# A decoder layer with experts on one core: the end of routing rebuilt, its index partly moved among the first expert's work

## The chip, the cores and the metric

The kernel runs on one core of a Trainium2 chip. Its engines work side by side, each through its own instructions in order, and wait for each other by semaphores: TensorE (PE in the profile, its weight loads PEld), VectorE (DVE), ScalarE (ACT), GpSimd (POOL) and SyncE (SP), which issues most of the transfers; GpSimd issues the indirect ones. The metric is the time of one execution in device microseconds; lower is better.

## What is computed

One layer: differential attention with a residual (the first 600 us, not touched here), then an RMS norm and a mixture of experts. For each of 1024 tokens a group of four experts is chosen by the largest group logit, then two experts inside it; their outputs are added, weighted:

```python
logit_g = (xt @ w_group + b_group).astype(F32)
prob_g = jax.nn.softmax(logit_g, -1)
g_sel = jnp.argmax(logit_g, -1)
gate_g = jnp.take_along_axis(prob_g, g_sel[:, None], -1)
logit_e = (xt @ w_router + b_router).astype(F32).reshape(n_tok, N_GROUPS, EXPERTS_PER_GROUP)
logit_e = jnp.take_along_axis(logit_e, g_sel[:, None, None], 1)[:, 0]
top_v, top_i = lax.top_k(jax.nn.softmax(logit_e, -1), TOP_K_IN_GROUP)
top_v = top_v / jnp.sum(top_v, -1, keepdims=True)
...
    h = jax.nn.silu(jnp.einsum('nd,edf->nef', xt, w_gate[e])) * jnp.einsum('nd,edf->nef', xt, w_up[e])
    h = h * combine[:, g, :, None].astype(h.dtype)
    y = y + jnp.einsum('nef,efd->nd', h, w_down[e])
```

There are 16 experts; the model width is 1024, an expert's 512.

## The kernel before

**Routing.** The tokens come in eight tiles of 128 (t = 0 to 7). For each, `logits` multiplies on TensorE, and `route_b` (L649) works on VectorE from the logits to `sel`, the one-hot pair of chosen experts, and then to the two weights, which it writes into the last 16 columns of xn, the normalised tokens; xn goes to the DRAM table `xn_dram`, 1040 columns wide. `route_r` (L696) turns `sel` into ranks by two small matmuls (rk) with a running count. `index_masks` (L151) compares the ranks with the slots: per expert a 128 x 128 mask pm, and one for the remainders (each expert has 140 slots, 128 and 12). `index_add` (L169) multiplies the masks with token numbers on TensorE (ix) and adds the result into ia (experts) and ir (remainders). `gather_index` (L192) makes from them the row numbers gidx, and `scatter_index` (L199) the rows sidx where results are added to the output.

**The order at the end of routing.** The order is written out by hand. In `last` (L885, t = 7) masks of tile 6 that wait in a list are put one by one between the steps of `route_b` (`Interleaved`, L619). `FIRST` names the two experts whose masks and index are made early, because the first gathers need them; the masks of the other 14 come after. `warm_up` issues matmuls whose result nobody reads. `start(part)` runs pieces of the expert stage early: 6 is the gathers for the first two experts and the first remainder block (`gather`, `gather_rem`), 2 is the first low half, 4 a weight load.

**The experts.** Each has three matrices (gate, up, down) in two tiles of 1 MB, 96 tiles in a fixed order: gate 0, up 0, gate 1, down 0, up 1, gate 2, down 1 and so on, two tiles each. A tile is loaded into `raw` (eight in flight); ScalarE rounds it to the high half mH (`split_h`, L1009), and VectorE subtracts that to get the low half mL (`split_l`, L1018). For each tile TensorE makes the high products with xT (L1088) and the low ones with xb (L1094) into two PSUM tiles (gu, three buffers of this kind). A matrix's second tile begins with its low products. `add_halves` then copies on ScalarE and adds on VectorE (L1115): gt for the gate (followed by silu), ut for up, yT for down; `hidden` (L1163) multiplies gt by ut and splits the product into hx and hb. `prepare(g)` (L1121), called after tile g's products and what follows them, splits halves ahead: high ones five tiles, low ones four (`LA = 4`; three in the last third), and loads into the freed raw buffer. `xpose(n)` transposes the gathered tokens of expert n, whose parts ScalarE and VectorE then put into xT and xb. The rest of the index (`other_experts`, L954) runs inside the first expert's first gate tile.

## Time and profile before

| | |
|---|---|
| median of 3 runs | 1005.19 us (1004.71 to 1005.73) |
| profiled execution | 1005.15 us, its span 1003.4 us |
| busy: PE, DVE, ACT, POOL | 941.4 (94%), 806.6 (80%), 748.5 (75%), 325.7 (32%) us |

The span is what the profile covers; 1.75 us of the execution's time lie around it. Busy time by stretch (end of attention's output; end of routing; first expert; the experts after it):

| stretch, us | length | PE busy | DVE busy | ACT busy | PE clock granted | DMA share |
|---|---|---|---|---|---|---|
| 596 to 620 | 24 | 23.82 | 18.95 | 9.95 | 1.00 | 0.89 |
| 620 to 635 | 15 | 9.57 | 13.30 | 9.32 | 0.89 | 0.52 |
| 635 to 658 | 23 | 20.20 | 21.59 | 15.07 | 1.00 | 0.97 |
| 658 to 679 | 21 | 20.40 | 20.39 | 19.33 | 1.00 | 0.78 |
| 679 to 701 | 22 | 21.69 | 20.07 | 20.40 | 1.00 | 0.98 |

An engine that is busy almost all of a stretch sets its length, or waits for the one that does. In a timeline a row is one or several like instructions in a row: start, time to the end of the last, engine, line, operation, output <- input with their shapes, and the count; in brackets stands how long the engine was idle before it and what ended that.

### The profile page before, as it was taken

What the parts mean: (1) busy time and instruction counts of PE and PEld (TensorE: products, weight loads), DVE (VectorE), ACT (ScalarE), POOL (GpSimd) and SP (SyncE); (2) the same over time, 40 slices, a digit from 0 to 9 for tenths busy, and PEclk for the clock granted to TensorE, in tenths of its full rate; (3) what the DMA queues carried; (4) which work ended last, traced back from release to release, by engine and by line L of the source; (5) the groups of instructions that cost most, each with busy time, mean ns of one, the idle gap of its engine ahead of it and who ended that gap; (6) DMA issues with size and microseconds to landing.
All of it is one profiled execution on the core that took longest, in us unless ns stands there. A gap on an engine that the chain in (4) does not pass through costs nothing. (4 is left out here: it accounts for less than half of the span.)

```text
span 1003.4 us, 19948 instructions
## 1 busy us (share of the span) xinstructions
PE 941.4 (94%) x7241; PEld 877.4 (87%) x7241; DVE 806.6 (80%) x1719; ACT 748.5 (75%) x1577; POOL 325.7 (32%) x977
## 2 busy tenths in 40 slices
PE   8989999999999999997899998899999999999992
PEld 7879999999999999987788886789999999999981
DVE  5578878888888888885677778999899899789880
ACT  6778877878877878776643325599999999899971
POOL 3533433415352432526744521301121312121011
PEclk8999999999999999998999999999999999999996
DMA  6230110202020110311323377889999999999923
GB/s 215 85 67 1 50 36 1 85 2 85 1 64 23 33 53 2 126 47 55 116 80 117 122 271 271 299 304 323 344 343 343 337 357 348 333 334 328 336 58 53
DMA packets 75771, 161.72 MB, mean 161 GB/s; under 512 B 8713, under 2 KB 39441, under 8 KB 67473
## 3 DMA queue, kind: packets, MB, share of 16 engines
q1 hardware_dynamic: 70544, 141.87, 39.7%
q0 software_dynamic: 5120, 18.50, 7.9%
q8 instruction: 59, 0.97, 0.4%
q14 instruction: 48, 0.39, 0.1%
HBM read 139.05 MB, written 21.30 MB: 160 GB/s over the span
## 5 line engine op out<-in xcount | busy, mean ns | idle before, releaser
L310 PE MATMUL qkv<-wH,hT 128*128 128x384 f32 x1024 | 293.3, 349 | 1.7 <-ACT wH L243 1.2
L1022 DVE TENSOR_TENSOR mL<-raw,mH 128x2048 bf16<-128x2048 f32 x95 | 215.7, 2283 | 3.7 <-ACT mH L1013 3.6
L310 PEld LDWEIGHTS qkv<-wH,hT 128*128 128x128 f32 x1024 | 190.5, 191 | 4.1 <-DVE vHL L323 2.4
L1013 ACT ACTIVATE mH<-raw 128x2048 fp32r<-128x2048 f32 x95 | 177.9, 1903 | 1.2 <-POOL rs_x L57 1.2
L310 PE MATMUL qkv<-wL,hT 128*128 128x384 f32 x512 | 173.6, 339 | 0.4 <-DVE wL L244 0.4
L1088 PE MATMUL gu<-xT,mH 128*128 128x280 f32 x1024 | 155.8, 299 | 4.1 <-DVE gt L1115 1.7
L1088 PEld LDWEIGHTS gu<-xT,mH 128*128 128x128 f32 x1024 | 136.3, 189 | 4.6 <-DVE gt L1115 1.9
L405 ACT ACTIVATE st<-st,nm 128x256 f32<-128x256 f32 (+7 forms) x128 | 99.2, 775 | 51.0 <-DVE nm L401 50.2
L1219 POOL DMA_INDIRECT out_dram<-yo,sidx x20 | 31.8, 1590 | 279.4 <-ACT yo L1217 244.8
L1094 PEld LDWEIGHTS <-mL 128*128 128x128 bf16 x1536 | 93.4, 97 | 10.6
L310 PEld LDWEIGHTS qkv<-wL,hT 128*128 128x128 f32 x512 | 98.0, 191 | 0.7 <-DVE wL L244 0.7
L401 DVE CUSTOM_DVE_ANT_0 st<-sc,bias 128x256 f32<-128x256 f32 (+7 forms) x128 | 93.7, 752 | 2.4 <-PE sc L393 0.3
L426 DVE TENSOR_TENSOR pdL<-tp,pdH 128x512 bf16<-128x512 f32 (+2 forms) x96 | 50.5, 554 | 49.6 <-ACT pdH L425 49.5
L561 PE MATMUL op<-wo,oH 128*128 128x512 f32 x256 | 82.5, 404 | 2.8 <-ACT oH L546 2.0
L1088 PE MATMUL gu<-hx,mH 128*128 128x280 f32 x512 | 82.2, 303 | 2.4 <-DVE yT L1115 1.8
L334 POOL TENSOR_SCALAR ssq<-ssq 128x8 f32<-128x8 f32 x32 | 7.1, 221 | 225.3 <-DVE ssq L326 224.7
L1094 PE MATMUL gu<-xb,mL 128*128 128x140 bf16 x1024 | 80.1, 225 | 0.0
L1088 PEld LDWEIGHTS gu<-hx,mH 128*128 128x128 f32 x512 | 68.9, 189 | 4.3 <-DVE yT L1115 3.3
L392 PE MATMUL sc<-KM,AH 128*128 128x384 f32 (+4 forms) x192 | 65.1, 345 | 2.3 <-DVE KM L367 2.3
L393 PE MATMUL sc<-KM,AL 128*128 128x384 f32 (+4 forms) x192 | 64.7, 343 | 0.5 <-DVE AL L369 0.5
L561 PEld LDWEIGHTS op<-wo,oH 128*128 128x128 f32 x256 | 47.9, 193 | 12.8 <-ACT oH L546 2.2
L412 DVE SCALAR_TENSOR_TENSOR st<-st,sm,st 128x128 f32<-128x128 f32 (+3 forms) x64 | 52.5, 820 | 2.2
(238 smaller groups left out, 1961.4 us busy)
## 6 DMA issues: line engine op xcount, KB each, us to landing
raw<-in_moe_w_gate_dram SPq DMA_DIRECT2D x32, 1024.0 KB, 8.1
raw<-in_moe_w_up_dram SPq DMA_DIRECT2D x32, 1024.0 KB, 6.8
raw<-in_moe_w_down_dram SPq DMA_DIRECT2D x31, 1024.0 KB, 8.4
wraw<-in_da_w_in_dram SPq DMA_DIRECT2D x64, 192.0 KB, 3.2
out_dram<-xres SPq DMA_DIRECT2D x9, 512.0 KB, 3.9
xraw<-in_x_dram SPq DMA_DIRECT2D x8, 512.0 KB, 6.1
woraw<-in_da_w_out_dram SPq DMA_DIRECT2D x8, 512.0 KB, 3.9
xres<-in_x_dram SPq DMA_DIRECT2D x8, 512.0 KB, 4.5
```

Source lines behind the costliest of these rows:

```text
L310: pe.matmul(ps, lhsT=hT[t][:, x, c], rhs=W[w, h, c // 3][:, c % 3], start=(c == 0 and x == 0 and w == "H"), stop=(c == 7 and x == 1))
L392: pe.matmul(ps[:, k, :wc], lhsT=AH[h, t][:, c], rhs=KM[h][:, c, ks], start=True, stop=False)
L393: pe.matmul(ps[:, k, :wc], lhsT=AL[h, t][:, c], rhs=KM[h][:, c, ks], start=False, stop=True)
L401: vec.tensor_tensor_reduce(sv, tiles[c][:, :n, :wc], bv, -1.0, 3e38, OP.add, OP.min, nm[:, c:c + 1])
L405: act.activation(st[c][:, :w], st[c][:, :w], AF.Exp, scale=-1.0, bias=nm[:, c:c + 1], accum_out=sm[:, c:c + 1])
L412: vec.scalar_tensor_tensor(st[0][:, :w], st[1][:, :w], sm[:, 3:4], st[0][:, :w], op0=OP.mult, op1=OP.add)
L426: vec.tensor_sub(pl[:, g:g + n], ps[:, :n], f(ph[:, g:g + n]))
L561: pe.matmul(ps, lhsT=o[:, c], rhs=wo[4 * half + c // 2][:, w, c % 2], start=(c == 0 and o is oh and w == 0), stop=(c == NK - 1 and o is ol))
L1013: act.activation(WH[g], full[g], AF.Copy)
L1022: vec.tensor_sub(WL[g], full[g], f(WH[g]))
L1088: pe.matmul(res[i // 2][:, i % 2, :2 * CAP], lhsT=wh[:, c - c0, 128 * i:128 * i + 128], rhs=rhs[:, c].rearrange("p a b -> p (a b)"), start ...
L1094: pe.matmul(res[i // 2][:, i % 2, :CAP], lhsT=wl[:, c - c0, 128 * i:128 * i + 128], rhs=rb[:, c], start=False, stop=(last and (c0 == 0 or ...
```

## The change

At the end of routing (`last`), the masks of tile 6 no longer stand between the steps of `route_b` for tile 7 but behind it. `route_b` ends at `sel` and hands back `weights`, which now runs behind the first low half. The index of tiles 6 and 7 for the first two experts and the remainders is made in one go: each pair of matmuls adds up in PSUM (`ahead`). The first gathers take only the 1024 columns of xn, by an index multiplied by the row width (gx); the weights go to a table of their own (`wt_dram`) and are gathered from there later (`start(7)`). The output's write comes before the norm's end instead of behind the weights.

In the experts' stage the other 14 masks of tile 7 (`flush`, now `rest[0]`) run behind two low halves, and the rest of the index (`rest[1]`), the third expert's gather and the weights' gathers run at the end of up's second tile of the first expert. Low halves are made two tiles ahead up to tile 5, three up to tile 17, and from tile 18 as before.

```diff
@@ def index_add @@
+        both = [(t, pm)] if ahead is None else [ahead, (t, pm)]
         for r in parts:
             for e in r:
-                pe.matmul(ps[:, e], lhsT=pm[:, e * 128:e * 128 + 128], rhs=tokp[:, t], start=True, stop=True)
+                for u, m in both:
+                    pe.matmul(ps[:, e], lhsT=m[:, e * 128:e * 128 + 128], rhs=tokp[:, u], start=(u == both[0][0]),
+                              stop=(u == t))
...
@@ def gather_index @@
+        if apart and lo in AT:
+
+            vec.tensor_scalar(gx[:p, AT[lo]:AT[lo] + 1], u[:, :1], float(XW), None, op0=OP.mult)
+            return lambda: gather_index(lo, hi, False)
         vec.tensor_copy(gidx[:p, lo:hi], u)
...
@@ def route_b @@
-        iv.scalar_tensor_tensor(s[:, 5:6], s[:, 4:5], 1.0, s[:, 1:2], op0=OP.add, op1=OP.mult)
-        iv.reciprocal(s[:, 5:6], s[:, 5:6])
-        iv.tensor_mul(s[:, 6:7], s[:, 5:6], s[:, 4:5])
-        iv.tensor_scalar(c2, iota16, i2[:, 1:2], s[:, 6:7], op0=OP.is_equal, op1=OP.mult)
-        iv.scalar_tensor_tensor(xn[:, D:], o1, s[:, 5:6], c2, op0=OP.mult, op1=OP.add)
...
+        def weights():
+
+            v = vec if t == NT - 1 else iv
+            v.scalar_tensor_tensor(s[:, 5:6], s[:, 4:5], 1.0, s[:, 1:2], op0=OP.add, op1=OP.mult)
+            v.reciprocal(s[:, 5:6], s[:, 5:6])
+            v.tensor_mul(s[:, 6:7], s[:, 5:6], s[:, 4:5])
+            v.tensor_scalar(c2, iota16, i2[:, 1:2], s[:, 6:7], op0=OP.is_equal, op1=OP.mult)
+            v.scalar_tensor_tensor(xn[:, D:], o1, s[:, 5:6], c2, op0=OP.mult, op1=OP.add)
+            sp.dma_start(wt_dram[t * 128:(t + 1) * 128], xn[:, D:])
+
+        if t == NT - 1:
+            R[t] = sel
+            return weights
+        weights()
...
@@ def last @@
-        x_sum = xr[t]
+        sp.dma_start(out[t * 128:(t + 1) * 128], xr[t])
         times_gain(t, x2, slice(64, 128))
         vec.scalar_tensor_tensor(ss[:, 1:2], ss[:, 1:2], -0.5 / D, ss[:, 0:1], op0=OP.mult, op1=OP.add)
         R[t] = xn, rsqrt_half(ss[:, 1:2])
+        route_r(t - 1)
+        first, rest = fill[:3], fill[3:]
+        fill.clear()
+        weights = route_b(t)
         start(3)
-        route_r(t - 1)
-        rest = fill[3:]
-        del fill[3:]
-        route_b(t)
-
-        sp.dma_start(out[t * 128:(t + 1) * 128], x_sum)
         start(5)
-        flush()
         warm_up(6)
-        route_i(t - 1, 0)
+
+        for do in first:
+            do()
         route_r(t)
         for _ in range(3):
             fill.pop(0)()
-        route_i(t, 0)
-        for e in FIRST:
-            gather_index(e, e + 1)
-        gather_index(NE, NE + 4)
+        index_add(t, R["pm", t], psQ, "po", False, 0, 1, (t - 1, R["pm", t - 1]))
+        later = [gather_index(e, e + 1) for e in FIRST] + [gather_index(NE, NE + 4)]
         start(6)
 
         warm_up(10)
         for do in rest:
             do()
         route_i(t - 1, 1)
-        flush()
 
         start(2)
         start(4)
+        weights()
+        sp.dma_start(xn_dram[t * 128:(t + 1) * 128, D:], R["xn"][:, D:])
         warm_up(8)
+
+        masks = flush
 
         def other_experts(ps_pool):
 
             index_add(t, R["pm", t], ps_pool, "gu", False, 1, 3)
             for r in REST:
                 gather_index(r[0], r[-1] + 1)
+            for do in later:
+                do()
             scatter_index()
 
         es_ps.close()
-        return other_experts
+        return masks, other_experts
...
@@ def moe_round @@
+            def rows(x, m, col, what=None):
+
+                dst, src = {None: (x[:m], xn_dram[:, :]), 0: (x[:m, :D], xn_dram.rearrange("t (d o) -> (t d) o", o=1)),
+                            1: (x[:m, D:], wt_dram[:, :])}[what]
+                ix = gidx[:m, col:col + 1] if what != 0 else gx[:m, AT[col]:AT[col] + 1]
+                pool.indirect_dma_start(out=dst, out_offset=None, in_=src,
+                                        in_offset=bass.IndirectOffsetOnAxis(ap=ix, axis=0))
...
-            pos, done_h, done_l = [0], [LA + 1], [LA]
+            pos, done_h, done_l = [0], [LA + 1], [3]
...
                 high(g + lead)
-                while done_l[0] <= g + lead:
+
+                lead_l = 2 if g < 6 else min(lead, 3) if g < 18 else lead
+                while done_l[0] <= g + lead_l:
                     split_l(done_l[0])
                     load(done_l[0] + NR)
                     done_l[0] += 1
...
-            def up(n, first, second):
+            def up(n, first, second, then=None):
                 def hidden():
...
                         vec.tensor_sub(hx[:, qs, 1], ut[i], f(hx[:, qs, 0]))
+                    if then:
+                        then()
...
-            xpose_rem(0)
+            gates = xpose_rem(0)
...
-            for g in (1, 2, 3):
+            for g in (1, 2):
                 split_l(g)
                 load(g + NR)
+            if rest:
+                rest[0]()
...
-            gate(0, lambda: rest(ps) if rest else None)
+            gate(0)
             for n in range(NE - 1):
-                if n + 2 < NE:
-                    gather(n + 2)
-                    if n % 4 == 1 and n + 3 < NE:
-                        gather_rem((n + 3) // 4)
-                up(n, lambda: xpose(n + 1), None)
+                if n == 0 and rest:
+                    up(0, lambda: xpose(1), None, lambda: (rest[1](ps), gather(2), start(7)))
+                else:
+                    if n + 2 < NE:
+                        gather(n + 2)
+                        if n % 4 == 1 and n + 3 < NE:
+                            gather_rem((n + 3) // 4)
+                    up(n, lambda: xpose(n + 1), None)
```

First place: VectorE at the end of routing, from the instruction behind the selection of the last token tile on. rs and k16 are the weights' parts, xn_8438 the tokens, pm the masks (pm_8519 of tile 6, pm_8586 of tile 7), rk1 and rank1 the rank, ia and ir the index. Before:

```order
L624 SCALAR_TENSOR_TENSOR rs_8525<-rs_8525 128x1
L624 RECIPROCAL rs_8525<-rs_8525 128x1
L624 TENSOR_TENSOR rs_8525<-rs_8525 128x1
L624 TENSOR_SCALAR k16_8532<-iota16_85,i2_8531,rs_8525 128x16
L624 SCALAR_TENSOR_TENSOR xn_8438<-k16_8532,rs_8525 128x16
L188 TENSOR_TENSOR ia_92<-ix_8569,ia_92 128x4 x2
L190 TENSOR_TENSOR ir_93<-ix_8569,ir_93 48x16
L703 TENSOR_TENSOR rk1_8582<-rk_8579,cnt1_91 128x16
L704 TENSOR_TENSOR rank1_90<-rk1_8582,sel_8533 128x16
L705 TENSOR_TENSOR cnt1_91<-rk_8579,cnt1_91 128x16
L158 TENSOR_SCALAR pm_8586<-slot1_84,rank1_90 128x128 x2
L162 TENSOR_TENSOR pm_8586<-slot1_84,rank1_90 128x192
```

In the changed kernel, in the same place (pm_8527 is tile 6's, pm_8579 tile 7's):

```order
L161 TENSOR_SCALAR pm_8527<-slot1_85,rank1_91 128x128 x2
L165 TENSOR_TENSOR pm_8527<-slot1_85,rank1_91 128x192
L723 TENSOR_TENSOR rk1_8575<-rk_8572,cnt1_92 128x16
L724 TENSOR_TENSOR rank1_91<-rk1_8575,sel_8540 128x16
L725 TENSOR_TENSOR cnt1_92<-rk_8572,cnt1_92 128x16
L161 TENSOR_SCALAR pm_8579<-slot1_85,rank1_91 128x128 x2
L165 TENSOR_TENSOR pm_8579<-slot1_85,rank1_91 128x192
L197 TENSOR_TENSOR ia_93<-ix_8583,ia_93 128x4 x2
L199 TENSOR_TENSOR ir_94<-ix_8583,ir_94 48x16
```

The five weight instructions and the first set of index additions have left; the three masks of tile 6 stand there instead, and one set of index additions is left.

Second place: VectorE in the first expert, around the up matrix. mL is a low half, gt, ut and hx the first expert's gate, up and hidden values, xT_8865 the next expert's tokens. Before; mL_8857 is the low half of tile 5:

```order
L1022 TENSOR_TENSOR mL_8811<-raw_8107,mH_8560 128x2048
L1115 TENSOR_TENSOR gt_8849<-gu_8746,gt_8849 128x280
L1115 TENSOR_TENSOR gt_8850<-gu_8747,gt_8850 128x280
L1022 TENSOR_TENSOR mL_8857<-raw_8370,mH_8815 128x2048
L1071 TENSOR_TENSOR xT_8865<-tp_8867,xT_8865 128x4x128
L1071 TENSOR_TENSOR xT_8865<-tp_8872,xT_8865 128x4x128
L1077 TENSOR_TENSOR xT_8865<-xr_8714,xT_8865 128x8x12
L1022 TENSOR_TENSOR mL_8918<-raw_8372,mH_8916 128x2048
L1115 TENSOR_TENSOR ut_8959<-gu_8863,ut_8959 128x280
L1168 TENSOR_TENSOR ut_8959<-gt_8849,ut_8959 128x280
```

In the changed kernel, from the low half of tile 4 on:

```order
L1046 TENSOR_TENSOR mL_8882<-raw_8114,mH_8560 128x2048
L1148 TENSOR_TENSOR ut_8923<-gu_8827,ut_8923 128x280
L1203 TENSOR_TENSOR ut_8923<-gt_8815,ut_8923 128x280
L1148 TENSOR_TENSOR ut_8924<-gu_8828,ut_8924 128x280
L1203 TENSOR_TENSOR ut_8924<-gt_8816,ut_8924 128x280
L1208 TENSOR_TENSOR hx_8921<-ut_8923,hx_8921 128x2x140
L1208 TENSOR_TENSOR hx_8921<-ut_8924,hx_8921 128x2x140
L197 TENSOR_TENSOR ia_93<-ix_8937,ia_93 128x12
```

Behind hx come the index additions and the row numbers, and then, at the end of the index:

```order
L219 TENSOR_TENSOR sidx_96<-ixs_8969 128x16
L217 SCALAR_TENSOR_TENSOR ixs_8973<-ir_94 48x4
L218 TENSOR_SCALAR ixs_8973<-ir_94,dump_88 48x4
L219 TENSOR_TENSOR sidx_96<-ixs_8973 48x4
L1046 TENSOR_TENSOR mL_8982<-raw_8378,mH_8781 128x2048
L1046 TENSOR_TENSOR mL_9022<-raw_8380,mH_8880 128x2048
L1148 TENSOR_TENSOR gt_9060<-gu_8988,gt_9060 128x280
```

The low half of tile 5 (now mL_8982) has moved from ahead of ut to behind ut, hx and eighteen instructions of the index; sidx is the last of these.

## Rows read from the trace of the kernel before

**Rows 1.** VectorE's timeline, 608 to 612 us: start us, us, instruction, times

```profile
608.54 0.24 DVE L624 SCALAR_TENSOR_TENSOR lg<-lg,rs_x,b 128x20 f32<-128x20 f32 x1
...
611.07 0.15 DVE L624 SCALAR_TENSOR_TENSOR rs<-rs 128x1 f32<-128x1 f32 x1
```

**Rows 2.** VectorE's timeline, 618 to 628 us

```profile
619.02 0.23 DVE L624 SCALAR_TENSOR_TENSOR lg<-lg,rs_h,b 128x20 f32<-128x20 f32 x1
...
621.75 0.15 DVE L624 SCALAR_TENSOR_TENSOR rs<-rs 128x1 f32<-128x1 f32 x1
...
623.03 0.15 DVE L703 TENSOR_TENSOR rk<-rk,cnt 128x16 f32<-128x16 f32 x1
...
623.43 0.42 DVE L158 TENSOR_SCALAR pm<-slot,rank 128x128 bf16<-128x128 bf16 x2
623.76 0.35 DVE L162 TENSOR_TENSOR pm<-slot,rank 128x192 bf16<-128x192 bf16 x1
624.53 0.23 DVE L188 TENSOR_TENSOR ia<-ix,ia 128x4 f32<-128x4 f32 x2 [0.41 <-PE ix L181]
...
625.51 2.40 DVE L158 TENSOR_SCALAR pm<-slot,rank 128x128 bf16<-128x128 bf16 x14
```

**Rows 3.** GpSimd's timeline, the first gather

```profile
626.00 1.39 POOL L1030 DMA_INDIRECT xg<-xn_dram,gidx  x1 [11.85 <-DMA out_dram<-xres]
```

**Rows 4.** TensorE's timeline, start of the first expert

```profile
631.14 1.07 PE L1065 MATMUL tp<-ident,xg 128*128 128x128 f32 x8 [0.75 <-DMA xg<-xn_dram,gidx]
...
634.92 1.30 PE L1088 MATMUL gu<-xT,mH 128*128 128x280 f32 x8 [1.30 <-DVE xT L1077]
```

**Rows 5.** VectorE's timeline, 631 to 658 us

```profile
631.15 2.28 DVE L1022 TENSOR_TENSOR mL<-raw,mH 128x2048 bf16<-128x2048 f32 x1
...
634.80 6.68 DVE L1022 TENSOR_TENSOR mL<-raw,mH 128x2048 bf16<-128x2048 f32 x3
...
641.41 0.26 DVE L188 TENSOR_TENSOR ia<-ix,ia 128x12 f32<-128x12 f32 x2
...
643.21 2.27 DVE L1022 TENSOR_TENSOR mL<-raw,mH 128x2048 bf16<-128x2048 f32 x1
...
653.03 0.44 DVE L1115 TENSOR_TENSOR ut<-gu,ut 128x280 f32<-128x280 f32 x1
...
655.67 2.35 DVE L1025 TENSOR_TENSOR mL<-raw,mH 128x1024 bf16<-128x1024 f32 x2
```

**Rows 6.** ScalarE's timeline, 633 to 653 us

```profile
633.41 0.28 ACT L1076 ACTIVATE xT<-xr 128x96 fp32r<-128x96 f32 x1
...
642.25 1.28 ACT L1155 ACT_TABLE_LOAD   x1
645.88 0.80 ACT L1155 ACTIVATE gt<-gt 128x280 f32<-128x280 f32 x2 [2.34 <-DVE gt L1115]
...
652.58 0.68 ACT L1113 ACTIVATE ut<-gu 128x280 f32<-128x280 f32 x2
```

**Rows 7.** Waits of TensorE, 634 to 700 us: us in total, times, longest

```profile
PE gu L1088 <- DVE gt L1115: 2.3, 2, 1.7
PE gu L1088 <- DVE xT L1077: 1.3, 1, 1.3
PE gu L1088 <- DVE ut L1115: 1.1, 1, 1.1
```

**Rows 8.** TensorE's timeline, second expert, two tiles apart

```profile
689.24 1.28 PE L1088 MATMUL gu<-xT,mH 128*128 128x280 f32 x8
...
695.54 1.29 PE L1088 MATMUL gu<-xT,mH 128*128 128x280 f32 x8
```

**Rows 9.** VectorE's timeline, second expert

```profile
687.63 0.80 DVE L1115 TENSOR_TENSOR yT<-gu,yT 128x280 f32<-128x280 f32 x2
```

**Rows 10.** TensorE's timeline in the attention part

```profile
468.76 2.11 PE L483 MATMUL tp<-ident,ou 128*128 128x128 f32 x8 [4.23 <-POOL ou L475]
```

**Rows 11.** Length; busy PE, PEld, DVE, ACT, POOL; clock; DMA share; GB/s

```profile
468.70:473.80 5.10, 5.04 (x19) 4.77 (x20) 1.66 (x5) 3.19 (x6) 3.94 (x17) 0.50 0.00 0
```

More of the change, by code (lines that the diff above doesn't have):

```diff
@@ L82, in trunk_layer_kernel @@
     xn_dram = dram.tile([T, XW], F32, name="xn_dram")
+    wt_dram = dram.tile([T, NE], F32, name="wt_dram")
     xin = a["x"].rearrange("b (t p) d -> (b t) p d", p=128)
@@ L149, in trunk_layer_kernel @@
     FIRST, REST = order[:2], (range(1, 4), range(5, NE))
+    AT = {e: i for i, e in enumerate(FIRST + [NE])}
     def index_masks(t):
@@ L167, in index_masks, with index_add @@
         return pm, [lambda e=e: main(e) for e in FIRST] + [rem] + [lambda e=e: main(e) for r in REST for e in r]
-    def index_add(t, pm, ps_pool, tag, first, part=None, bufs=1):
+    def index_add(t, pm, ps_pool, tag, first, part=None, bufs=1, ahead=None):
         ps = ps_pool.tile([128, NE + 4, 4], F32, name="ix", tag=tag, bufs=bufs)
         parts = {None: [range(NE)], 0: [range(e, e + 1) for e in FIRST], 1: REST}[part]
+        both = [(t, pm)] if ahead is None else [ahead, (t, pm)]
         for r in parts:
             for e in r:
-                pe.matmul(ps[:, e], lhsT=pm[:, e * 128:e * 128 + 128], rhs=tokp[:, t], start=True, stop=True)
+                for u, m in both:
+                    pe.matmul(ps[:, e], lhsT=m[:, e * 128:e * 128 + 128], rhs=tokp[:, u], start=(u == both[0][0]),
+                              stop=(u == t))
         if part != 1:
             for b in range(4):
-                m = NE * 128 + b * 4 * REM
-                pe.matmul(ps[:4 * REM, NE + b], lhsT=pm[:, m:m + 4 * REM], rhs=tokp[:, t], start=True, stop=True)
+                c = NE * 128 + b * 4 * REM
+                for u, m in both:
+                    pe.matmul(ps[:4 * REM, NE + b], lhsT=m[:, c:c + 4 * REM], rhs=tokp[:, u], start=(u == both[0][0]),
+                              stop=(u == t))
         if first:
@@ L851, in trunk_layer_kernel @@
             routing_constants()
+            sp.dma_start(xn_dram[(NT - 1) * 128:, D:], iota16)
         if t == 2 and 0 <= h < H - 1:
@@ L1025, in split_l, with gather, gather_rem @@
                         vec.tensor_sub(WL[g][:, 2 * i:2 * i + 2], r, f(WH[g])[:, 2 * i:2 * i + 2])
-            def gather(n):
-                e = order[n]
-                x = w_tile([128, XW], F32, "xg")
-                pool.indirect_dma_start(out=x, out_offset=None, in_=xn_dram[:, :],
-                                        in_offset=bass.IndirectOffsetOnAxis(ap=gidx[:, e:e + 1], axis=0))
-                X["g", n] = x
-            def gather_rem(b):
-                x = w_tile([128, XW], F32, "xgr")
-                pool.indirect_dma_start(out=x[:4 * REM], out_offset=None, in_=xn_dram[:, :],
-                                        in_offset=bass.IndirectOffsetOnAxis(ap=gidx[:4 * REM, NE + b:NE + b + 1], axis=0))
-                X["gr", b] = x
+            def rows(x, m, col, what=None):
[4 more added lines that the diff above has]
+                                        in_offset=bass.IndirectOffsetOnAxis(ap=ix, axis=0))
+            def gather(n, what=None):
+                if what != 1:
+                    X["g", n] = w_tile([128, XW], F32, "xg")
+                rows(X["g", n], 128, order[n], what)
+            def gather_rem(b, what=None):
+                if what != 1:
+                    X["gr", b] = w_tile([128, XW], F32, "xgr")
+                rows(X["gr", b], 4 * REM, NE + b, what)
             def xpose_rem(b):
@@ L1158, in gate @@
                 res = results()
-                half(res, xT, xb, 0, NK, behind)
-                half(res, xT, xb, 4, NK, silu)
-            def up(n, first, second):
+                half(res, xT, xb, 0, NK)
+                half(res, xT, xb, 4, NK, lambda: (silu(), behind and behind()))
+            def up(n, first, second, then=None):
                 def hidden():
@@ L1240, in start @@
                 else:
-                    gather(0)
-                    gather_rem(0)
-                    gather(1)
+                    what = part - 6
+                    gather(0, what)
+                    gather_rem(0, what)
+                    gather(1, what)
             for g in range(5):
@@ L1306, in next_index @@
                 index_add(t, pm, psi, "ix", t == 0)
-        gather_index(0, NE)
-        gather_index(NE, NE + 4)
+        for lo, hi in [(e, e + 1) for e in FIRST] + [(r[0], r[-1] + 1) for r in REST] + [(NE, NE + 4)]:
+            do = gather_index(lo, hi)
+            if do:
+                do()
         scatter_index()
-        for part in range(7):
+        for part in range(8):
             start(part)
```

23 lines of the change are left out of this document (13 added, 10 removed).

## The prediction

> **What bounds the kernel now.** I read the page first, then the busy times of five stretches (both in the table above). TensorE is busy 94% of the span and stays near 100% up to 620 us; it is down to 9.57 of 15 us between 620 and 635, and 20.20 of 23 us between 635 and 658. The change touches only these places, and VectorE is the busiest engine in both (13.30 of 15, 21.59 of 23). So TensorE sets the time, and what it loses here it loses to VectorE, which works in order. The second view was VectorE's timeline at the end of routing [rows 1, 2], with GpSimd's and TensorE's beside it [rows 3, 4]: one chain runs from the last logits through selection, rank, masks, index and gather to the first expert's first matmul at 634.92. The third was VectorE's and ScalarE's timeline in the first expert [rows 5, 6], with TensorE's waits there [rows 7]: 1.3 us for xT, 2.3 us for gt in two waits, 1.1 us for ut. Names: tile k is the k-th half matrix of the experts (0, 1 gate; 2, 3 up; 4, 5 the next expert's gate; 6, 7 down), L k and H k its low and high half, T the start of tile 0.
>
> **The end of routing.** Uninterleaved, the step from the logits to the instruction after the selection took 611.07 - 608.54 = 2.53 us for the token tile before [rows 1]; for the last one, with three masks in between, 621.75 - 619.02 = 2.73 [rows 2]. Gain 0.2. Behind the selection stood the weights and three index additions, 623.03 - 621.75 = 1.28 us. They go away, and the three masks taken out of the chain come in their place: from 623.43 to 623.76 + 0.35 = 624.11, that is 0.68. Gain 0.6. Rank and masks of the last tile stay at 1.08 us (623.03 to 624.11). TensorE then has eight rather than four small matmuls ahead of the index additions, which come 0.42 us after the last mask now (624.53); double would be 0.42 more, none 0; the first half can run before the last mask, so I take 0.15. The three factors XW replace three conversions one for one. So the gather, which started at 626.00 [rows 3], starts about 0.65 earlier. Its row puts that start down to the write of the output, but in the program the gather waits for the writes of xn_dram, for the index and for an old buffer, not for that transfer. It starts 1.47 after the first index addition (624.53), with four instructions of about 0.15 between; so at most 0.9 of that can be the output write, and I give nothing for writing it earlier.
>
> The gather's rows land 5.14 us after its start (631.14) [rows 3, 4], before as after. Next VectorE was in the way: L0 ran from 631.15 to 633.43 [rows 5], while ScalarE had the last part of xT ready at 633.41 + 0.28 = 633.69 [rows 6], and yet tile 0 started only at 634.92, 1.2 us later. In the change the last tile's 14 masks go behind L2, so L0 is done before the rows land; only the five weight instructions, at most 1.28 us, stand between, and end about with ScalarE's first copy. I take 0.95 of the 1.2, since the last subtraction itself stays. Sum: T comes 1.6 us earlier. Bounds: 0.65 (L0's place gives nothing) and 2.5 (0.9 more from the output write).
>
> **The first expert, what goes.** L3 moves from ahead of gt to behind it, and the index and L4 behind that too. VectorE then has after T: L1 and L2 (2.23 each; three took 6.68 [rows 5]), 14 masks (2.40 in the other group [rows 2]), free at T + 6.8. A tile takes TensorE 3.15 us: the same place two tiles on is 695.54 - 689.24 = 6.30 later [rows 8]. So tile 1 ends at T + 6.3 and gt follows at once: both waits for gt go, 2.3 us [rows 7].
>
> **What comes: tile 4.** ScalarE's order is unchanged: table load 1.28, silu, xT of the next expert, H6, H7, then ut. The table load can start at about T + 7.0, so silu at T + 8.3; silu to ut was 652.58 - 645.88 = 6.70 [rows 6], so ut's copy comes at T + 15.0 and VectorE's first addition, 0.45 later as before (653.03 [rows 5]), at T + 15.4, done at T + 15.9. TensorE has ended four tiles, eight transposes (about 0.9 apart from the rest, 1.07 as a row [rows 4]) and 14 index matmuls (0.4) at T + 13.9. Before, tile 4 began in a free PSUM buffer and only its second half waited for ut (the 1.1 us); now the index takes that buffer last, and tile 4's first half waits for the first ut addition. So 1.1 goes and 2.0 comes.
>
> **What comes: tile 5.** It begins with low-half products, which need L5. Before, L5 was done ahead of ut (second order place). Now VectorE does, from ut's first addition at T + 15.4: ut and hx, 655.67 - 653.03 = 2.64; the index, 643.21 - 641.41 = 1.80 for twelve instructions and, with six more at the same mean of 0.15, 2.7 [rows 5]; then L5, 2.23. That is T + 23.0. TensorE has done tile 4 at T + 15.9 + 3.15 = T + 19.05. It stands for 3.9 us. The bounds: a shorter ut chain on ScalarE cannot start before tile 3 ends, which takes at most 1.1 off (2.8); six index instructions at 0.3 add 0.9 (4.8).
>
> **Two extra splits.** With the lead of two raised to three at tile 6 and to four at tile 18, VectorE there does two low halves where it did one, between two sets of yT additions. Before, the addition at 687.63 ended its first half 0.4 later, 1.2 us before TensorE needed it at 689.24 [rows 8, 9]. With 2.23 more it comes 1.0 late. Two places: 2.0 us; none if VectorE is ahead there, 4.5 if nothing hides. Beyond tile 22 the order is that of before.
>
> **Nothing for the rest.** Loads are issued behind their low half, two tiles later than before at first, but still five tiles (16 us) ahead of use. The weights' small gathers start at about T + 22, and the first use is at T + 35; even at twice the 5.14 us of a large gather they are there. The gather for the third expert starts at T + 20 and is used at T + 33. SP's eight small writes stand where it waited before. If the third gather came late, TensorE would pay one for one.
>
> **Sum.** Gone: 1.6 + 2.3 + 1.1 = 5.0. Added: 2.0 + 3.9 + 2.0 = 7.9. Net +2.9 on the profiled execution's 1005.15, which is the median of 1005.19: 1008.1. The extremes, 2.5 + 3.4 gone with 3.7 added (0.9 at tile 4, 2.8 at tile 5), and 0.65 + 3.4 gone with 13.8 added (tiles 4 and 5 at 6.8, splits 4.5, clock 2.5), are -2.2 and +9.8.
>
> **Clock.** Earlier in this trace TensorE stood for 4.23 us before 468.76 [rows 10]; after that its clock was granted at 0.50, the 1.2 GHz level, for 5.1 us in which it was busy for 5.04 [rows 11]. So 2.5 us were lost behind the wait. The waits up to 1.7 us here show no such thing. 3.9 us lies near the one that did.
> The Trainium skill (TensorE: Matmul & The Clock Gate, "Why this matters for your kernels") warns of idle gaps between bursts of matmuls: they put the engine back to its lower clock. Rows 10 and 11 agree; by that rule the rival named next would be the forecast.
>
> **Rivals.**
> - The clock falls in the wait at tile 5. For: rows 10 and 11. Against: 3.9 is the shorter wait, and tile 4 runs at full rate just before. Price 2.5, of which the later yT waits give back about 0.6, since VectorE gains on TensorE: 1010.0.
> - ut comes sooner on ScalarE (H6 and H7 done in a gap). Each us takes one off tile 4's wait and VectorE's whole chain; at the bound, 1.1 at tile 5 and 1.1 of the splits, 1005.9. Against: the order has H6 and H7 ahead.
> - No wait at tile 5, the one on the other side: VectorE reaches the index 3.9 us sooner than I place it, because the deferred low halves and the early T leave it idle. Then 3.9 goes, 1004.2, and with VectorE ahead the splits' 2.0 too: 1002.2. It decides from about 3 us on. For: VectorE has a gap before ut in my walk. Against: that gap is ScalarE's, and the chain behind ut is 7.6 us long in rows against 3.65 for TensorE.
>
> **Chances.** My forecast 0.42 (own range 1006.8 to 1009.4); clock 0.16; ut sooner 0.27; no wait at tile 5 0.15. Range 1004.0 to 1010.6: it leaves out most of the last and the top of the second. A change within 0.2% (2 us, 1003.2 to 1007.2) can't be told from none. Faster 0.15 (the last); same 0.28 (the third and a sliver of the first); slower 0.57.
>
> **What would show it.** In the new profile: the first gather about 0.65 us earlier and tile 0 about 1.6 earlier; TensorE waits of about 2 us for ut ahead of tile 4 and about 4 for mL, put down to VectorE, ahead of tile 5, with the index instructions of 2.7 us between hx and mL on VectorE; no wait for gt in the first expert; about 1 us for yT at tiles 8 and 20. I am wrong if the wait for mL is under 1 us, if the clock drops after it (then the second case), or if TensorE gains more than 2.5 us before tile 0.

## The result: 5.9 us slower, and the profile after

The changed kernel takes 1011.37 us (median of five runs, 1005.92 to 1013.01) where the kernel before takes 1005.19 on the same chip. The ratio is 1.0059, with a 95% interval of 1.0039 to 1.0079: 5.9 us slower (3.9 to 7.9). Slower was forecast, by 2.9 us; the time lies above the range.

The profiled execution of the changed kernel is the one of 1005.92, the fastest of the five, with a span of 1004.2, and a look at the spans alone (1003.4 before) would find no loss. The reason lies ahead of the change. The last selection (`sel`) came at 621.59 in the kernel before and at 616.06 in this execution, and between 613.29 and 622.63 in the traces of this study, after nearly the same code: the clock falls at other moments in each. Ahead of `sel` it stood at 0.50 for 23.9 us in the one and for 13.7 us in the other. So every trace is read from `sel`. From there to the first of the last transposes it is 983.76 - 621.59 = 362.17 us before and 984.10 - 616.06 = 368.04 after: 5.87 more, as much as the runs lost. The forecast counts from the last logits, 2.57 us ahead of `sel` before (619.02 [rows 2]) and 2.36 in the changed kernel (613.70); by its count the loss is 0.21 less, 5.66.

Routing's end first, in VectorE's, GpSimd's and TensorE's timelines of the changed kernel (start us, us, instruction, times, in brackets idle before and what ended it):

```profile
613.70 0.23 DVE L637 SCALAR_TENSOR_TENSOR lg<-lg,rs_h,b 128x20 f32<-128x20 f32 x1
...
616.06 0.23 DVE L637 SCALAR_TENSOR_TENSOR sel<-iota,i,k 128x16 bf16<-128x16 f32 x1
```

```profile
619.79 1.23 POOL L1056 DMA_INDIRECT xg<-xn_dram,gidx  x1 [10.84 <-DVE pm L161]
```

```profile
624.99 1.06 PE L1098 MATMUL tp<-ident,xg 128*128 128x128 f32 x8 [0.67 <-DMA xg<-xn_dram,gidx]
627.86 1.30 PE L1121 MATMUL gu<-xT,mH 128*128 128x280 f32 x8 [0.41 <-DVE xT L1110]
...
643.73 1.30 PE L1121 MATMUL gu<-xT,mH 128*128 128x280 f32 x8 [1.89 <-DVE ut L1148]
...
650.87 1.11 PE L1127 MATMUL gu<-xb,mL 128*128 128x140 bf16 x8 [3.75 <-DVE mL L1046]
651.74 4.08 PE L1121 MATMUL gu<-xT,mH 128*128 128x280 f32 x16
655.62 0.94 PE L1127 MATMUL gu<-xb,mL 128*128 128x140 bf16 x8
656.37 1.28 PE L1121 MATMUL gu<-hx,mH 128*128 128x280 f32 x8
...
665.78 1.30 PE L1121 MATMUL gu<-xT,mH 128*128 128x280 f32 x8 [0.43 <-DVE yT L1148]
...
684.04 1.30 PE L1121 MATMUL gu<-hx,mH 128*128 128x280 f32 x8 [1.23 <-DVE yT L1148]
...
728.64 1.31 PE L1121 MATMUL gu<-hx,mH 128*128 128x280 f32 x8 [1.22 <-DVE yT L1148]
```

The gather starts 3.73 us behind `sel`, where it was 4.41 [rows 3]; tile 0 starts 11.80 behind it, where it was 13.33 [rows 4]. So 1.53 us are gained, or 1.74 from the last logits on. Then the five rows with large brackets: 1.89 for ut at tile 4, 3.75 for L5 at tile 5, and for yT 0.43 in tile 8, 1.23 in tile 13 and 1.22 in tile 25 (a tile is 32 matmuls of L1121 and L1127; the expectations below call this one tile 19). The waits for gt and the second-half wait for ut [rows 7] are gone. Tile 5 itself is odd: it takes from 650.87 to 656.37, 5.50 us, and its 16 large matmuls 4.08, where they take 2.31 elsewhere.

The stretches around it show why (length; busy us of TensorE, its loads, VectorE, ScalarE, GpSimd; granted clock; DMA share; GB/s):

```profile
646.00:649.50 3.50, 1.13 (x13) 0.88 (x12) 3.26 (x19) 3.50 (x2) 1.90 (x3) 0.98 0.25 40
649.50:656.00 6.50, 5.13 (x28) 5.00 (x29) 3.97 (x3) 0.45 (x2) 5.89 (x3) 0.50 0.81 276
656.00:659.00 3.00, 3.00 (x31) 2.93 (x29) 1.96 (x3) 2.21 (x4) 1.17 (x2) 0.97 0.97 373
```

TensorE stopped at 647.1; from 649.4 to 656.2 its clock was granted at 0.50, the 1.2 GHz level. Against 3.15 us for a tile at full clock that is 2.35 us lost.

VectorE's rows of the same place tell it from the other side:

```profile
643.22 0.45 DVE L1148 TENSOR_TENSOR ut<-gu,ut 128x280 f32<-128x280 f32 x1 [2.15 <-ACT ut L1146]
...
645.87 0.27 DVE L197 TENSOR_TENSOR ia<-ix,ia 128x12 f32<-128x12 f32 x2
...
648.54 4.48 DVE L1046 TENSOR_TENSOR mL<-raw,mH 128x2048 bf16<-128x2048 f32 x2
654.43 0.45 DVE L1148 TENSOR_TENSOR gt<-gu,gt 128x280 f32<-128x280 f32 x1 [1.42 <-ACT gt L1146]
657.04 0.45 DVE L1148 TENSOR_TENSOR gt<-gu,gt 128x280 f32<-128x280 f32 x1 [2.16 <-ACT gt L1146]
```

Three brackets matter. VectorE stands idle for 2.15 us ahead of ut, though L5 could be made there; then it works through ut, hx and the index (645.87 to 648.54) while TensorE waits for that same L5; and then it stands for gt twice, 3.58 us, because tile 5 starts late and crawls. Together that is 5.73 us of idle time. Against the kernel before, which idles in other places, VectorE's idle time has grown by 4.56 us and its work by 1.33 (the account below). That reading is theory D below.

### The profile page after: what moved, and what is told of

It reads as the page before. It is cut to its first block, busy times and chain, and to the rows that moved or that the text cites. A ratio compares the mean times of both kernels' runs of the same rounds, so it can differ in the third digit from the quotient of the medians.

```text
span 1004.2 us, 19968 instructions
## 1 busy us (share of the span) xinstructions
PE 940.1 (94%) x7241; PEld 876.3 (87%) x7241; DVE 803.5 (80%) x1722; ACT 748.7 (75%) x1577; POOL 333.6 (33%) x980
## 5 line engine op out<-in xcount | busy, mean ns | idle before, releaser
L1121 PE MATMUL gu<-xT,mH 128*128 128x280 f32 x1024 | 157.6, 302 | 2.8 <-DVE ut L1148 1.9
L1121 PEld LDWEIGHTS gu<-xT,mH 128*128 128x128 f32 x1024 | 138.0, 191 | 3.8 <-DVE ut L1148 2.0
L1127 PEld LDWEIGHTS <-mL 128*128 128x128 bf16 x1536 | 94.0, 98 | 14.7 <-DVE mL L1046 3.9
L1121 PE MATMUL gu<-hx,mH 128*128 128x280 f32 x512 | 82.2, 303 | 3.8 <-DVE yT L1148 3.3
L1127 PE MATMUL gu<-xb,mL 128*128 128x140 bf16 x1024 | 80.8, 226 | 3.7 <-DVE mL L1046 3.7
L1121 PEld LDWEIGHTS gu<-hx,mH 128*128 128x128 f32 x512 | 68.9, 189 | 5.2 <-DVE yT L1148 4.2
```

The lines of the kernel that those rows point to most:

```text
L1121: pe.matmul(res[i // 2][:, i % 2, :2 * CAP], lhsT=wh[:, c - c0, 128 * i:128 * i + 128], rhs=rhs[:, c].rearrange("p a b -> p (a b)"), start ...
L1127: pe.matmul(res[i // 2][:, i % 2, :CAP], lhsT=wl[:, c - c0, 128 * i:128 * i + 128], rhs=rb[:, c], start=False, stop=(last and (c0 == 0 or ...
```

## Experiments

All are counted from `sel` to the first of the last transposes, in one trace each, beside the timed ratio to the kernel before where one was taken. Two ways of reckoning compete in them. S: TensorE's waits are prices that add up, as the forecast took them; with it goes theory A on what the prices are (the wait at tile 5, the clock behind it, the extra splits). D: up to tile 25 (19 in the expectations) VectorE's queue is the bound, a wait of TensorE is only where that shows, and what counts is VectorE's work and its idle time.

**1. L5 ahead of ut.**

```diff
-                lead_l = 2 if g < 6 else min(lead, 3) if g < 18 else lead
+                lead_l = 3 if g == 2 else 2 if g < 6 else min(lead, 3) if g < 18 else lead
```

> The changed kernel, but low half 5 is made right behind low half 4, ahead of ut of tile 3, where VectorE idled 2.15 us (641.06 to 643.22) in the changed kernel's trace; low half 6 follows as there. Theory A (the loss is the wait at tile 5 plus the clock it costs, 3.75 + 2.35 us, and 2.2 us of later waits on yT that come from the two extra splits behind tiles 6 and 18): the wait of 3.75 us at tile 5 is gone or under 0.5, the granted clock stays at 1.00 there, the wait for ut stays near 1.9 to 2.0; 6.1 us less than the changed kernel, so about 0.2 us below the kernel before (-0.5 to +0.5). The yT waits of 1.2 us at tiles 13 and 19 stay. Theory B (the later yT waits are the echo of the stall at tile 5): they go as well, 8.3 us less, 2.4 us below the kernel before.

Measured: ratio 1.0012 (0.9996 to 1.0028); 362.29 us, 5.75 less than the changed kernel. VectorE's timeline:

```profile
639.96 4.49 DVE L1046 TENSOR_TENSOR mL<-raw,mH 128x2048 bf16<-128x2048 f32 x2
644.40 0.45 DVE L1148 TENSOR_TENSOR ut<-gu,ut 128x280 f32<-128x280 f32 x1
```

and TensorE's:

```profile
644.90 1.29 PE L1121 MATMUL gu<-xT,mH 128*128 128x280 f32 x8 [1.90 <-DVE ut L1148]
646.04 0.67 PE L1127 MATMUL gu<-xb,mL 128*128 128x140 bf16 x8
646.52 1.28 PE L1121 MATMUL gu<-xT,mH 128*128 128x280 f32 x8
647.64 1.16 PE L1127 MATMUL gu<-xb,mL 128*128 128x140 bf16 x16
```

The idle time ahead of ut is filled, ut comes as soon as before (1.90), tile 5 follows tile 4 without a gap, and the clock reads 1.00. Nearly the whole loss hangs on one low half of 2.28 us and its place in the queue. The yT waits at tiles 13 and 25 stayed (1.24 and 1.23), so theory B falls.

**2. The wait at tile 5 filled.** The added matmuls write a PSUM tile (the kind that matmuls write) that nothing reads.

```diff
+                if g == 5 and X.get("fill"):
+                    w = ps.tile([128, 512], F32, name="tp", bufs=2)
+                    for _ in range(X.pop("fill")):
+                        pe.matmul(w, lhsT=before, rhs=ones[:, None, :].to_broadcast([128, 4, 128]), start=True, stop=True)
```

> The changed kernel with 15 added matmuls (128x512 bf16, 0.21 us apart in the trace, 3.2 us in all) into an unused PSUM tile between tiles 4 and 5, where TensorE waits 3.75 us for low half 5. Theory A (the clock falls because TensorE stands still there): the wait stays, filled; the granted clock stays at 1.00 from 646 to 657 and tile 5 takes 3.15 us, not 5.5; 2.35 us less than the changed kernel, about 3.5 us above the kernel before. Rival C (the clock falls for what went before, whatever TensorE does there): the clock still reads 0.50 for some 6 us; time as the changed kernel's, 5.9 us above the kernel before, or a little more.

Measured: ratio 1.0049 (1.0030 to 1.0069); 366.35 us, 1.69 less than the changed kernel, not 2.35. The clock did not fall in tile 5, but it fell in tile 4, behind the wait for ut:

```profile
640.00:643.50 3.50, 1.60 (x29) 1.45 (x27) 1.30 (x3) 3.19 (x5) 0.00 (x0) 1.00 0.78 276
643.50:647.00 3.50, 3.50 (x20) 3.37 (x21) 3.19 (x16) 3.03 (x5) 0.30 (x1) 0.55 0.54 208
647.00:651.00 4.00, 4.00 (x27) 2.43 (x27) 3.90 (x9) 2.25 (x2) 3.39 (x3) 0.97 0.47 135
```

Tile 4 took 4.78 us in place of some 3.2, so the fill ended 0.9 behind L5, and the time alone did not decide between A and C.

**3. Two ahead to the end; 4. the same with L5 ahead of ut.**

```diff
+                lead_l = 2                            # 3
+                lead_l = 3 if g == 2 else 2           # 4
```

> The changed kernel with low halves two tiles ahead to the end: the extra splits behind tiles 6 and 18 do not take place, and raw weights are loaded up to two tiles later. Theory A (the extra splits make VectorE late for ut, so ScalarE's chain of hx, high halves, gt and yT late): the waits for yT at tiles 13 and 19 fall from 1.2 us each to 0.2 to 0.3, and that at tile 8 goes; 2.2 us less than the changed kernel, 3.7 us above the kernel before. Theory B (echo of the stall at tile 5): the waits stay; 5.9 us above. If the later loads bind, a wait for raw shows in ScalarE's high halves and the time is above the changed kernel's.

> The edits of the first and third kernel together: low half 5 ahead of ut, two tiles ahead to the end. Theory A: 6.1 + 2.2 = 8.3 us less than the changed kernel, 2.4 us below the kernel before (-3.0 to -1.8). Theory B: the same as the first kernel alone by its own reckoning (2.4 below), with the first kernel there already; if the first kernel stands at -0.2 and this one at -2.4, B falls.

Measured: ratios 1.0201 (1.0173 to 1.0230) and 1.0164 (1.0137 to 1.0190); 382.78 and 376.55 us. Both far off. The waits of TensorE in the first of them, 630 to 1000 us (us in total, times, longest):

```profile
PE gu L1127 <- DVE mL L1046: 26.3, 15, 3.7
PE gu L1121 <- DVE ut L1148: 1.9, 1, 1.9
...
PE tp L1249 <- DVE yT L1148: 0.3, 1, 0.3
```

The yT waits of the products did go, as A said. But with a lead of two the wait at the second gate tile, which the changed kernel has once, comes back in every expert, 1.6 us each behind the first: the low half for that tile always stands behind ut and hx. The extra splits are what ends that. In the first of the two kernels the beginning, up to tile 6, is that of the changed kernel, and it repeats it: 3.74 us of wait at tile 5, and the clock at 0.50 for 6.8 us.

**5. Both waits filled.** Experiment 2 with 8 more of its matmuls in the wait for ut ahead of tile 4.

```diff
-                if g == 5 and X.get("fill"):
+                if g in (4, 5) and X.get("fill"):
...
-                    for _ in range(X.pop("fill")):
+                    for _ in range(X["fill"].pop(0)):       # 8, then 15
```

> The second experiment with 8 more of the added matmuls ahead of tile 4, where TensorE waits 1.9 us for ut. There the clock did not fall in tile 5 any more, but for 3.3 us in tile 4. Theory A (it falls for the waits): with both waits filled it reads 1.00 from tile 0 to 660 us; tile 4 takes 3.24 us again and tile 5 3.15; 368.0 less 2.35 = 365.7 us from sel to the last transposes, with the wait for low half 5 itself still there. Rival C: it falls all the same, 366.3 to 368.

```profile
648.00:652.00 4.00, 4.00 (x37) 3.16 (x36) 3.62 (x21) 3.94 (x6) 1.05 (x2) 1.00 0.34 129
652.00:656.00 4.00, 3.49 (x26) 2.18 (x25) 3.97 (x4) 1.19 (x1) 3.69 (x2) 1.00 0.51 141
```

365.50 us, 2.54 less than the changed kernel (one run, 1007.31 us). The clock read 1.00 from tile 0 on. C falls: the waits bring the clock down, and it costs 2.35 to 2.54 us.

**6. One extra split, not two.** Low halves three ahead from tile 6 to the end, L5 ahead of ut.

```diff
+                lead_l = 3 if g == 2 or g > 5 else 2
```

> The first experiment (low half 5 ahead of ut) and low halves three tiles ahead from tile 6 to the end, so that the second extra split (behind tile 18) does not take place; the first (behind tile 6) stays. All counted from the last selection (sel) to the first of the last transposes, which was 362.2 us in the kernel before, 368.0 in the changed one, 362.3 in the first experiment. Theory A (each extra split makes VectorE late for ut, and TensorE waits for yT about 1.05 us longer): the wait for yT at tile 19 falls from 1.23 to 0.17, as in the kernel before; 361.2. Rival B (the waits at tiles 13 and 19 come from something else that the first part of the change leaves behind): 362.3 again.

Measured: 361.18 us, as A said to 0.02; ratio 0.9988 (0.9959 to 1.0017). The wait for yT in tile 25 fell under what the view shows. An extra split costs 1.1 us here.

**7. Low halves as far ahead as before, all else as changed.**

```diff
-            pos, done_h, done_l = [0], [LA + 1], [3]
+            pos, done_h, done_l = [0], [LA + 1], [LA]
...
+                lead_l = lead
...
-            for g in (1, 2):
+            for g in (1, 2, 3):
...
-            gate(0)
+            gate(0, rest and rest[0])
```

> The changed kernel with the low halves as far ahead as in the kernel before (1 to 3 in front of tile 0, four ahead), and the masks behind gt; routing's end and the place of the rest of the index stay as changed. From sel to the last transposes. Theory D (from the selection to about tile 19 VectorE's work is the bound: what counts is how long it idles, 5.73 us more between these two in the changed kernel than in the first experiment and 0.0 more in the first experiment than in the first and third expectations' terms): VectorE has no idle of 2.15 ahead of ut and none in tile 5; the waits move to gt (2.3) and ut (4 to 5) and the sum comes out at 362.5 (362.0 to 363.0). Theory S (the waits of TensorE add up one by one, as the forecast reckoned): tile 0 1.5 earlier, ut 3.4 later, gt 0.6 less: 363.5. The clock may fall in a wait for ut of 4 us, which would add about 2.3 to either.

Measured: 362.59 us (D 362.5, S 363.5); ratio 1.0001 (0.9974 to 1.0027). TensorE's rows:

```profile
642.85 1.83 PE L1121 MATMUL gu<-xT,mH 128*128 128x280 f32 x8 [3.50 <-DVE ut L1148]
644.48 1.16 PE L1127 MATMUL gu<-xb,mL 128*128 128x140 bf16 x8
```

The wait for ut is 3.50 us and the clock fell in tile 4 here too (1.83 in place of 1.30), yet the end came no later: TensorE's lost time lay beside VectorE's queue. And routing's end, with tile 0 11.62 us behind `sel`, 1.7 sooner than before, shows no gain at the end of the count (362.59 against 362.17).

**8. The index sums' PSUM tile elsewhere** (one run, on top of 6).

```diff
-            index_add(t, R["pm", t], ps_pool, "gu", False, 1, 3)
+            index_add(t, R["pm", t], ps_pool, "tp", False, 1, 2)
```

> The kernel with one step (361.2 us from sel to the last transposes), but the PSUM tile of the other experts' index sums comes out of the transposes' two tiles and not out of the three of the products, so that tile 4 finds a free one and need not wait 1.9 us for ut. Theory D (VectorE's work is the bound to tile 19): tile 4 begins 1.9 us earlier and the waits behind it grow by as much, 361.2 (360.9 to 361.5). Theory S (waits of TensorE add up): 359.3.

```profile
645.95 1.29 PE L1121 MATMUL gu<-xT,mH 128*128 128x280 f32 x8
647.08 0.67 PE L1127 MATMUL gu<-xb,mL 128*128 128x140 bf16 x8
647.99 1.30 PE L1121 MATMUL gu<-xT,mH 128*128 128x280 f32 x8 [0.24 <-DVE ut L1148]
...
655.14 0.67 PE L1127 MATMUL gu<-hb,mL 128*128 128x140 bf16 x8 [1.15 <-DVE mL L1046]
```

Tile 4 starts 13.84 us behind tile 0 in place of 15.87, two us sooner, and the end comes at 361.05 in place of 361.18. The wait of 1.9 us was real and worth nothing: it came back as 0.24 for ut, 1.15 for a low half in tile 6, and more for yT. S falls, as far as one trace tells.

**9. L1 ahead of tile 0, the gate weights behind L2** (on top of 6). L0 goes to where VectorE waited 0.9 us for the index sums of the token tile before.

```diff
         for do in rest:
             do()
+        start(2)
         route_i(t - 1, 1)
-
-        start(2)
+        start(9)              # low half 1
         start(4)
-        weights()
-        sp.dma_start(xn_dram[t * 128:(t + 1) * 128, D:], R["xn"][:, D:])
         warm_up(8)
-        masks = flush
+        def masks():
+            weights()
+            sp.dma_start(xn_dram[t * 128:(t + 1) * 128, D:], R["xn"][:, D:])
+            flush()
```

> The previous kernel with one step, and at routing's end low half 0 put ahead of the index sum for which VectorE idled 0.9 us, low half 1 ahead of tile 0, and the last tile's gate weights (five small instructions, 1.15 us) behind low half 2. From sel to the last transposes. Theory D: VectorE's queue behind tile 0 is 1.1 us shorter: 361.2 less 1.1 = 360.1; tile 0 at most 0.3 later. Theory S (tile 0's start counts): 361.5.

Measured: 360.49 us, 0.7 less, of the 1.1 by D; ratio 0.9993 (0.9956 to 1.0030).

**10. Masks on GpSimd; 11. the index later as well.** In both, low halves 1 to 3 are made ahead of tile 0 and the lead is three from the start, with one more behind tile 2. 11 has the PSUM tile of 8, one more behind tile 4 too, and the first gates one expert later.

```diff
-            vec.tensor_scalar(pm[:, e * 128:e * 128 + 128], ...
+            (pool if t == NT - 1 and e not in FIRST else vec).tensor_scalar(
+                pm[:, e * 128:e * 128 + 128], ...
...
+                lead_l = 4 if g == 2 else 3           # 10
...
-                gate(n + 1)                           # 11
+                gate(n + 1, (lambda: (rest[1](ps), gather(2), start(7))) if n == 0 and rest else None)
```

> Low halves three ahead from the start (1 to 3 in front of tile 0; 5 and 6 ahead of ut of tile 3), no step later, and the last tile's 14 masks made on GpSimd (0.62 us each by its 128x128 multiplications, 8.7 in all, beside 23.5 us in which it idles) in place of VectorE (2.4 us). From sel to the last transposes. Theory D: 2.4 us less of VectorE's work and one low half less by tile 19, no idle added; what TensorE still waits for is ut at tile 4 (about 1.9): 359.5 (358.7 to 360.2), about 2.7 below the kernel before. If GpSimd's masks slow VectorE or come after tile 3: a wait for pm or longer low halves show, 361 or more.

Measured: 361.63 us, 2.1 more than expected; ratio 0.9988 (0.9964 to 1.0011). GpSimd's timeline, the 14 masks together and two pieces of them, with VectorE's low halves beside the second piece:

```profile
624.80 21.97 POOL L161 TENSOR_SCALAR pm<-slot,rank 128x128 bf16<-128x128 bf16 x14
```

```profile
626.87 2.34 POOL L161 TENSOR_SCALAR pm<-slot,rank 128x128 bf16<-128x128 bf16 x4
```

```profile
629.20 4.69 POOL L161 TENSOR_SCALAR pm<-slot,rank 128x128 bf16<-128x128 bf16 x1
```

```profile
629.02 6.78 DVE L1046 TENSOR_TENSOR mL<-raw,mH 128x2048 bf16<-128x2048 f32 x3
```

The 14 masks took 22 us, not 8.7. The 0.62 for one was nearly right: seven took 0.59 to 0.60 us and two 0.86. But each of the five that began while VectorE was making a low half took 2.08 to 4.69. The low halves took no longer for it (2.26 each). So the index matmuls ahead of tile 4 waited for masks, and behind that wait the clock fell in tile 4:

```profile
PE ix L183 <- POOL pm L161: 3.4, 3, 2.1
```

```profile
647.20:650.60 3.40, 3.40 (x21) 3.27 (x19) 3.16 (x20) 3.40 (x3) 1.92 (x2) 0.50 0.98 359
```

> The kernel with the masks on GpSimd, where they took 22 us and held up the index sums at tile 3: now the sums, their PSUM tile out of the transposes' two, and the rest of the index follow gt of tile 5, some 3 us after GpSimd's last mask; low halves four ahead behind tiles 2 and 4, else three; the first gates one expert later. Theory D: 2.4 us of masks and the second step's 2.3 us are off VectorE's queue and it does not idle over 0.5 us up to tile 6: TensorE waits neither for ut nor for masks, for yT 0.3 at most; 358 (357.3 to 359.5) us from sel to the last transposes, 4 below the kernel before. If the first gates or the third gather come too late, a wait for xg or cr shows at tile 8 or 13: 360 or more.

Measured: 358.78 us, 3.4 below the kernel before; ratio 0.9987 (0.9973 to 1.0000), 1002.44 us. TensorE's waits from 630 to 760 us:

```profile
PE tp L1098 <- DMA xg<-xn_dram,gidx: 0.7, 1, 0.7
PE gu L1121 <- DVE ut L1148: 0.7, 1, 0.7
PE tp L1077 <- ACT yo L1254: 0.6, 1, 0.6
...
```

No wait over 0.8 us is left in this stretch. It is the shortest of all by the trace; by the runs its gain of 1.3 us (0 to 2.7) touches the edge of what they can tell, and less than the trace shows.

**VectorE's account.** One row each of the kernel before, the changed one and 1, from `sel` to the yT additions of tile 24 (length; busy VectorE and its instructions; clock):

```profile
621.59:727.78 106.19, 96.64 (x161) 0.98 0.88 309
```

```profile
616.06:728.14 112.08, 97.97 (x166) 0.95 0.82 286
```

```profile
617.12:723.39 106.27, 97.78 (x167) 0.98 0.87 303
```

and the same for all, idle being length less busy:

| kernel | to the end | VectorE busy | idle | sum | rest to the end |
|---|---|---|---|---|---|
| before | 362.17 | 96.64 | 9.55 | 106.19 | 255.98 |
| changed | 368.04 | 97.97 | 14.11 | 112.08 | 255.96 |
| 1, L5 ahead of ut | 362.29 | 97.78 | 8.49 | 106.27 | 256.02 |
| 2, wait at tile 5 filled | 366.35 | 98.04 | 12.28 | 110.32 | 256.03 |
| 3, two ahead | 382.78 | 94.44 | 18.05 | 112.49 | 270.29 |
| 4, both | 376.55 | 94.12 | 12.12 | 106.24 | 270.31 |
| 5, both waits filled | 365.50 | 97.97 | 11.49 | 109.46 | 256.04 |
| 6, one extra split | 361.18 | 95.91 | 9.17 | 105.08 | 256.10 |
| 7, leads as before | 362.59 | 97.86 | 8.75 | 106.61 | 255.98 |
| 8, index sums' PSUM tile | 361.05 | 95.96 | 8.93 | 104.89 | 256.16 |
| 9, L1 ahead of tile 0 | 360.49 | 95.69 | 8.74 | 104.43 | 256.06 |
| 10, masks on GpSimd | 361.63 | 94.25 | 11.26 | 105.51 | 256.12 |
| 11, the index later | 358.78 | 94.22 | 8.41 | 102.63 | 256.15 |

The last column hardly moves, except in 3 and 4, whose lead stays at two behind that point. In front of it the idle time is 8.4 to 9.6 us in seven kernels (before, 1, 6, 7, 8, 9, 11), and their order is that of VectorE's work, to 0.2 us. In the other six it is 11.3 to 18.1. 10 has less work than 9 and yet ends 1.1 us later: behind the late tile 4 VectorE stands for gt, 2.6 us in two waits. Work and idle time add up to the length by definition, so the table shows where the time went. That VectorE's queue sets it is what 7, 8 and 9 speak for, each in one trace.

## Why the prediction was wrong

Step by step, in its own names:

- **Routing's end, 1.6:** from the last logits on, as the forecast counts, 1.74 (15.90 to 14.16), and the gather 0.89 earlier (forecast 0.65). 0.21 of each lies ahead of `sel`. Right within 0.25.
- **Waits for gt, 2.3 gone, and ut's second half, 1.1 gone:** neither is in the changed kernel's trace. Right.
- **Tile 4, 2.0 for ut:** 1.89, at T + 15.87 (forecast T + 15.9). Right.
- **Tile 5, 3.9 for L5:** 3.75, at T + 23.01 (forecast T + 23.0), with 2.67 us of index between hx and L5 (2.7). Right.
- **Two extra splits, 2.0:** three yT waits came to 2.88, where the kernel before had 0.31 and 0.17 in tiles 13 and 25: 2.4 more. The size was right within 0.4, the place hardly: not tiles 8 and 20 (0.43 and 0.11) but, for the most part, 13 and 25, each seven tiles behind its split. Without the second split the wait at 25 went (experiment 6). Theory A's reason, that a late VectorE makes ut late and with it ScalarE's chain to the next yT, fits that but was not tried by itself.
- **Clock, left out of the sum:** this step failed. The terms as measured, 1.74 + 2.3 + 1.1 gone and 1.89 + 3.75 + 2.4 added, give +2.9, the forecast. The clock's 2.35 makes +5.25, and the 5.66 counted from the last logits leave 0.4 for gaps too short for the view of waits.

The clock stood among the rivals, with its price nearly right (2.5 against 2.35) and a chance of 0.16, and its drop was named as a sign of being wrong. Two arguments held it down and neither bore weight. "3.9 is the shorter wait" set it 0.3 below the 4.23 of [rows 10]. But in the same trace of the kernel before the clock had fallen behind waits half as long, two in the attention part (TensorE's rows; length, busy times, clock, DMA):

```profile
56.44 0.41 PE L392 MATMUL sc<-KM,AH 128*128 128x384 f32 x1 [2.25 <-DVE KM L367]
...
487.38 1.00 PE L561 MATMUL op<-wo,oH 128*128 128x512 f32 x2 [1.98 <-ACT oH L546]
```

```profile
57.60:61.00 3.40, 3.40 (x12) 3.18 (x12) 2.14 (x8) 1.08 (x4) 0.00 (x0) 0.50 0.00 0
487.70:491.10 3.40, 3.21 (x10) 2.25 (x9) 2.78 (x7) 2.33 (x6) 3.21 (x5) 0.50 0.00 0
624.20:627.60 3.40, 3.40 (x12) 1.39 (x13) 2.97 (x22) 2.33 (x2) 1.39 (x1) 0.50 0.38 154
```

The third stretch lies behind waits of 1.53 and 1.67 us at routing's end, so "the waits up to 1.7 us here show no such thing" misread the trace as well; it is the 0.89 in the table of stretches. And the 0.6 that later waits were to give back did not come: with both waits filled, 2.54 us came back. With the rival's price added to the forecast and nothing given back it would have read 1010.6, within the ratio's interval.

The Trainium skill (TensorE: Matmul & The Clock Gate, "Why this matters for your kernels") had been weighed in the prediction, by whose rule this rival was the forecast. The trace agrees with it: 0.50 behind the 3.75 us of tile 5, in both kernels that have that wait unfilled (the changed one and 3).

There is a second fault, which did not move the sum. The forecast booked tile 0's 1.6 us as a gain and each wait as a loss. Experiments 7 and 8 speak against both, in one trace each: VectorE's queue runs on through them. The terms came out right because the walk along VectorE's queue was right, and that queue holds them all. Read that way, the change adds to VectorE's work (97.97 us against 96.64), takes away the low half that it could have made ahead of ut, and so leaves it idle for 2.15 us there; the late and slow tile 5 makes it wait 3.58 more. Of its idle time 2.6 us go when the clock holds (14.11 to 11.49 in experiment 5), and 5.6 when L5 stands ahead of ut (8.49 in experiment 1). The prediction saw that gap ("VectorE has a gap before ut in my walk") and used it only to weigh a rival; it did not ask what could stand in it.

What stays open: why the runs of 11 show 1.3 us of gain and the trace 3.4. The interval ends at 2.7; other executions may lose clock ahead of `sel` in other places, and that was not tried.

## What to carry to other kernels

Where one in-order engine feeds several waits of TensorE in a row, add up that engine's work and idle time from one common point to another, not TensorE's waits: a wait taken away comes back at the next place, and only idle time filled or work removed is gained. If a change leaves such an engine idle ahead of a slow producer, look for the instruction that the next wait will want, and put it there. And a new stall of TensorE should be held against all waits of the same trace behind which the clock fell, not the longest alone; where it is longer than most of them and TensorE has no slack there (it had in experiment 7), the clock's price belongs in the sum, not among the rivals.
